# Differential attention in groups of two steps, two sums moved to VectorE, a first load in halves: one change to a whole encoder layer

## The chip, the cores and the metric

The kernel runs on one core of a Trainium2 chip as one program. The metric is the device time of an execution in microseconds. The core has a matrix engine (TensorE, "PE" in the profile; its weight loads are "PEld"), a vector engine (VectorE, "DVE"), an activation engine (ScalarE, "ACT"), a general engine (GpSimd, "POOL") and a queue engine that issues the transfers (SyncE, "SP"). Every engine works through its own instructions in order and waits for the others by semaphores. TensorE writes into PSUM, which has eight banks of 128 x 512 floats.

## The reference

One layer of a hybrid encoder over two sequences of 512 tokens, width 1024, all in float32:

```python
def _layer(x, mem, l, p):
    xn = _rmsnorm(x, p['norm_mix'][l]); mn = _rmsnorm(mem, p['norm_mem'][l])
    u, q, k, v, xq, g = jnp.split(xn @ p['w_in'][l], IN_SPLITS, axis=-1)
    y_s5 = _s5_branch(u, ...)                      # state space branch
    y_diff = _diff_attention(q, k, v, lam, ...)    # q, k rotated
    mk, mv = jnp.split(mn @ p['w_mem_kv'][l], 2, axis=-1)
    y_x = _cross_attention(xq, mk, mv)
    merged = sum(sigmoid(g_n) * (branch_n @ p['w_up'][l, n]))
    x = x + merged @ p['w_out'][l]
    gate, up = jnp.split(_rmsnorm(x, p['norm_ffn'][l]) @ p['w_ffn_in'][l], 2, axis=-1)
    return x + (silu(gate) * up) @ p['w_ffn_out'][l]
```

The differential attention takes, for each of 4 heads, two score maps over 64 channels each, and weighs the values with their difference:

```python
s = jnp.einsum('bqhd,bkhd->bhqk', qblk, k) * scale
probs = softmax(s).reshape(Bn, DIFF_HEADS, 2, Q_BLOCK, L)
w = probs[:, :, 0] - lam * probs[:, :, 1]
out = jnp.einsum('bhqk,bkhe->bqhe', w, v)          # then an rmsnorm over each head's 128 channels
```

## The kernel before

Matrices are kept as two parts of reduced precision, a high part (names ending in h) and the rest (l), and a product is three products on TensorE: high with high, high with low, low with high. `split` (L131) makes the two parts: ScalarE copies the high part, VectorE subtracts it. The kernel is a sequence of stages, whose program order for TensorE is written out by hand while `PE.on` is set; the other engines' orders come from a scheduler at build time, which works with a timeline of its own.

**Start** (L304 to L322). `NWARM` products of zeros run on TensorE while the first transfers are under way. Then the first weight tile is loaded in two halves, and beside each half `mem_part(i)` (L222) loads a tile of two rows of the transposed memory (128 x 2 x 512) and splits each row. `mem_k(0, ...)` multiplies them in the order of the rows.

**Differential attention** (L819 to L922). There are 32 steps: 4 heads x 2 sequences x 4 query tiles of 128 tokens. For each step, `score(i)` (L832) issues six products on half of the rows (64 channels each), two at a time into two banks of the pool "sc", and then the softmax of both: VectorE takes the maximum (L543), ScalarE the exponential with its sum (L548), VectorE combines the two maps (L849, L850) into a tile e. `turn(i)` (L853) transposes e in four pieces into a bank of the pool "tr" and splits it from there: pH on ScalarE, pL on VectorE. `outputs(i)` (L864) multiplies two turned steps with the values, 12 products. After every fourth step `squares` (L884) and `normed` (L897) make the norm over the head's channels; each transposes through a "tr" bank as well.

Between these pieces `fill(n)` (L598) puts products of other work into TensorE's order: it takes units from `queue`, each of six products, until it has given n; what it gives too much is carried to the next call. The queue holds the projections of the next heads' queries and keys with their rotation (VectorE and GpSimd), a half of the values, four gate tiles, and the first two branches of the merge. `finish` draws a unit's generator to its end where a step needs it.

The PSUM pools in this stage are those of the cross attention before it (L584): mm=2 for the filler products, sc=3, tr=2, oo=1 for outputs.

The loop runs one step at a time: score(i + 1), fill, turn(i), outputs for every second step, fill, then squares and normed of earlier steps.

**Feed-forward** (L1057 to L1296). Both its halves multiply in seven instead of eight block products, which needs sums of quarter blocks. `quad_sums` (L966) makes the four sums of a pair of activation tiles: three on VectorE (L971, L973, L974) and one on GpSimd (L972), whose result lies in t_[:, 2]. `quad_split` (L983) splits a pair's tiles and sums. `act_pair` (L1117) loads two tiles that the first half has written to memory and makes their sums. At the seam between the halves, `acts` (L1146) prepares pairs 0 and 1 while the last tile's products run, `nxt` (L1244) pair 2; `pair_in` (L1183) the later ones. `quadrants` (L1104) empties the seven banks of a visit: a ScalarE copy of the first bank (L1107), then VectorE additions (L1101).

Of the kernel before, what the change touches and what calls it, by code (L numbers as in the profile page):

```python
# [14 lines left out]
ALU = mybir.AluOpType  # L15
# [25 lines left out]

NG = (7, 6, 3)

NWARM = 13

SCAN = (40, 47, 53, 60)
ROUND = 12582912.0
# [25 lines left out]
def encoder(ctx: ExitStack, tc: tile.TileContext, a, out):  # L73
    nc = tc.nc
# [18 lines left out]
    def open_banks(**tags):  # L93

        bank_es.close()
        for tag, n in tags.items():
            pools[tag] = bank_es.enter_context(tc.tile_pool(name=tag, bufs=n, space=PSUM, reuse_waits="tile"))
# [28 lines left out]
    def vcol(name, i=0):  # L126
        o = VEC[name][0] + i
        return vec[:, o : o + 1]


    def split(hi, lo, src, scale=None):  # L131

        if scale is None:
            h = S.copy(hi, src)  # L134
            l_ = V.tensor_tensor(out=lo, in0=src, in1=hi.bitcast(F32), op=ALU.subtract)  # L135
        else:
            h = S.activation(out=hi, in_=src, func=AF.Copy, scale=scale)
            l_ = V.scalar_tensor_tensor(out=lo, in0=src, scalar=scale, in1=hi.bitcast(F32), op0=ALU.mult, op1=ALU.subtract)
        return h, l_
# [81 lines left out]

    def mem_part(i):  # L222
        mt_ = slot("ld", [P, 2, L], name="mt")
        nc.sync.dma_start(mt_, a["memT"][:, 2 * i : 2 * i + 2, :])
        for j in range(2):
            split(mh[i][:, j, :], ml[i][:, j, :], mt_[:, j, :], scale=vcol("norm_mem", 2 * i + j))

    last_sq = None
# [369 lines left out]
    def fill(n):  # L598
        nonlocal owed
        owed += n  # L600
        while owed > 0 and queue:
            r = next(queue[0], None)
            if r is None:
                queue.pop(0)
            else:
                owed -= r
        if not queue:
            owed = 0
# [154 lines left out]
    def qk_units(h, is_q):  # L763
        qk[h, is_q], use = rotated(is_q)
        yield from units(a["w_in"][(4 if is_q else 8) + h], xh, xl, use)
# [53 lines left out]
    qk[0, True], use = rotated(True)  # L819
    for s in range(NS):  # L820
        use(s, dq0[s])
    for _ in qk_units(0, False):
        pass
    for _ in gate_units():
# [7 lines left out]
    def score(i):  # L832
        nonlocal last_e
        h, s, qt = steps[i]
        cs = slice(s * L, (s + 1) * L)
        if h and s == qt == 0:
            finish(dk[h])
        if qt == 0:
            s0[h, s] = acol.tile([P, 4], F32, tag="s0", name="s0", bufs=3)
        (qh, ql), (kh, kl), er = qk[h, True], qk[h, False], []  # L840
        qs_ = slice(s * L + qt * P, s * L + (qt + 1) * P)
        sc = [bank("sc") for _ in MAPS]
        for q_, k_ in ((qh, kh), (qh, kl), (ql, kh)):
            for o, rows in zip(sc, MAPS):
                PE.matmul(o, q_[rows, qs_], k_[rows, cs], start=(k_ is kh and q_ is qh), stop=(q_ is ql))
        for mp in range(2):
            er.append(softmax_parts(ap_, acol, sc[mp], L, 1.0, f"d{mp}", None if mp else s0[h, s][:, qt : qt + 1]))
        (e0, sm0), (e1, r1) = er
        V.scalar_tensor_tensor(out=r1, in0=r1, scalar=nlam, in1=sm0, op0=ALU.mult, op1=ALU.mult)  # L849
        last_e = last_x, V.scalar_tensor_tensor(out=e0, in0=e1, scalar=r1, in1=e0, op0=ALU.mult, op1=ALU.add)  # L850
        es[i] = e0

    def turn(i):  # L853
        h, s, qt = steps[i]
        if qt % 2 == 0:
            pT[h, s, qt // 2] = tuple(slot("pT", [P, 4, 2 * P], F32R, n_) for n_ in ("pH", "pL"))
        e0 = es.pop(i)
        tr = aux()
        for j in range(4):
            PE.transpose(tr[:, j * P : (j + 1) * P], e0[:, j * P : (j + 1) * P], ident)  # L860
        ps = slice(qt % 2 * P, qt % 2 * P + P)
        split(*(p_[:, :, ps] for p_ in pT[h, s, qt // 2]), tr.rearrange("p (j q) -> p j q", j=4))

    def outputs(i):  # L864

        h, s, qt = steps[i]
        if h == 2 and s == qt - 1 == 0:
            finish(v1_)
        vh, vl = (v1 if h >= 2 else v0)[s]
        vs = slice((h % 2) * P, (h % 2) * P + P)  # L870
        pH, pL = pT.pop((h, s, qt // 2))
        if qt == 1:
            osb[h, s] = bank("oo")
        od = osb[h, s][:, qt // 2 * 2 * P : (qt // 2 + 1) * 2 * P]
        for j in range(4):
            PE.matmul(od, vh[:, j, vs], pH[:, j, :], start=(j == 0), stop=False)
            PE.matmul(od, vh[:, j, vs], pL[:, j, :], start=False, stop=False)
            PE.matmul(od, vl[:, j, vs], pH[:, j, :], start=False, stop=(j == 3))
        if qt == 3:
            o_ = rp.tile([P, L], F32, tag="nsq", name="osb", bufs=2)  # L880
            S.copy(o_, osb[h, s])
            osb[h, s] = o_
# [14 lines left out]
    def normed(i):  # L897
        h, s, _ = steps[i]
        _, bc = factor(ss[h, s], P, bias=0.0)
        V.scalar_tensor_tensor(out=osb[h, s], in0=osb[h, s], scalar=g04, in1=bc, op0=ALU.mult, op1=ALU.mult)  # L900
        nc.sync.dma_start(bD[1, h, :, s * L : (s + 1) * L], osb[h, s])

    n = len(steps)
    for i in range(-1, n + 3):
        if i + 1 < n:
            score(i + 1)
        if i == 22:
            queue.insert(1, first_in())
        fill(10 if i < n - 1 else 16)
        if 0 <= i < n:  # L910
            turn(i)
        if 0 < i <= n and steps[i - 1][2] % 2:
            outputs(i - 1)
        fill(10)
        if 1 < i <= n + 1 and steps[i - 2][2] == 3:
            squares(i - 2)
        if i > 2 and steps[i - 3][2] == 3:
            normed(i - 3)
    aes.close()
    while queue:  # L920
        fill(24)
# [41 lines left out]

    last_p = None

    def quad_sums(xa_, xb_, tag="ts"):  # L966

        nonlocal last_p
        b11, b12, b21, b22 = xa_[:, 0:L], xa_[:, L:NT], xb_[:, 0:L], xb_[:, L:NT]
        t_ = slot(tag, [P, 4, L], name="ts")  # L970
        V.tensor_tensor(out=t_[:, 0], in0=b12, in1=b11, op=ALU.subtract)  # L971
        last_p = PO.tensor_tensor(out=t_[:, 2], in0=b22, in1=b12, op=ALU.subtract)  # L972
        V.tensor_tensor(out=t_[:, 1], in0=b22, in1=t_[:, 0], op=ALU.subtract)  # L973
        V.tensor_tensor(out=t_[:, 3], in0=b21, in1=t_[:, 1], op=ALU.subtract)  # L974
        return t_
# [138 lines left out]
        c21 = summed(other[0], next(ps), u3, 2)  # L1114
        return c11, summed(other[1], next(ps), u4, 2), c21, c22

    def act_pair(p, tag="ts"):  # L1117

        xa_, xb_ = slot("ld", name="fa"), slot("ld", name="fb")
        nc.sync.dma_start(xa_, aD[2 * p])  # L1120
        nc.sync.dma_start(xb_, aD[2 * p + 1])
        return xa_, xb_, quad_sums(xa_, xb_, tag)

    def all7(i):
        wg = weights4(i)
# [8 lines left out]
    for i in range(KFF):  # L1134
        w = nxt_w or all7(i)
        nxt_w = None
        if i == 1:
            prep = prepare(pes, pieces[NPREP[0] : NPREP[1]])
            next(prep)
        elif i == KFF - 3:  # L1140
            assert next(prep, None) is None
            pes.close()
            open_tags(fes, side="right", tsa=1, tsb=1)
        if i == KFF - 1:
            with tc.issue_after(last_s[1].ins):
                acts = [act_pair(0, "tsa"), act_pair(1, "tsb")]  # L1146
            PE.on = True

        ps = products(i, w)
        p0 = next(ps)  # L1150
        if i == 0:
            for s in range(NS):
                _, bc = rstd(accs[s], DM)
                S.copy(accs[s], bc)
        gf0, gf1, up0, up1 = quadrants(ps, p0)
        ac = ap2.tile([P, NT], F32, tag="ac", name="ac")
        with ExitStack() as es_:
            if i == KFF - 2:
                nxt_w = all7(i + 1)
                es_.enter_context(tc.issue_after(last_s[1].ins))  # L1160
            for s, gf, up in ((0, gf0, up0), (1, gf1, up1)):
                cs = slice(s * L, (s + 1) * L)
                V.tensor_tensor(out=gf, in0=gf, in1=accs[s], op=ALU.mult)
                last_t = S.activation(out=ac[:, cs], in_=gf, func=AF.Tanh, scale=0.5)
                PO.tensor_tensor(out=up, in0=up, in1=accs[s], op=ALU.mult)  # L1165
                V.scalar_tensor_tensor(out=ac[:, cs], in0=ac[:, cs], scalar=1.0, in1=gf, op0=ALU.add, op1=ALU.mult)
                V.tensor_tensor(out=ac[:, cs], in0=ac[:, cs], in1=up, op=ALU.mult)
        nc.sync.dma_start(aD[i], ac)
        if 1 <= i < KFF - 3:
            half_piece((last_t, last_sum))  # L1170
# [70 lines left out]
    next(coming[1])  # L1241
    next(coming[0], None)
    with queued():
        nxt = act_pair(2)  # L1244
    n_p = 0
    for v, (m, lo_, hi_) in enumerate(VISITS):
        ps = [bank() for _ in range(6)] + [aux()]
# [544 lines left out]
```

## Time and profile before

| what | us |
|---|---|
| median of three runs | 1605.7 |
| lowest and highest of them | 1605.64, 1608.26 |
| the profiled execution | 1606.34 |
| its span, first to last instruction | 1604.6 |

The profile is of one execution. A row of a timeline gives an instruction's start and duration in us, its engine and line, its operation, the tile that it writes and the tiles that it reads, its shape, and in brackets how long the engine stood idle before it and what ended that. Names are the program's own: bkmm, bksc, bktr and bkoo are banks of the four PSUM pools. TensorE's products overlap: one lasts about 0.39 us from its first input to its last result, but the next starts 0.23 us after it, so that its pace is read from the starts and its busy time hides small gaps.

### The profile page before, as it was taken

How to read it: one execution, taken by the hardware profiler on the slowest of the kernel's cores; microseconds unless marked ns; L12 is line 12 of the kernel's file. 1: busy time of each engine (PE TensorE's matmuls, PEld its weight loads, DVE VectorE, ACT ScalarE, POOL GpSimd, SP SyncE). 2: the span in 40 equal slices, each digit the busy share in tenths (PEclk: the TensorE clock that was granted, in tenths of full speed). 3: DMA queues.
4: the chain of work that ended last, by engine and by line, in shares of the span. 5: the costliest groups of instructions: out<-in, count | busy, mean ns of one | idle time of the engine just before them, and what ended most of it. 6: DMA issues, size and time to landing. Idle time of an engine off the chain costs nothing.

```text
span 1604.6 us, 21632 instructions
## 1 busy us (share of the span) xinstructions
PE 1587.0 (99%) x7838; PEld 1313.2 (82%) x7838; DVE 1163.7 (73%) x1854; ACT 639.7 (40%) x1142; POOL 557.8 (35%) x451
## 2 busy tenths in 40 slices
PE   9999999999999999999999999999999999999997
PEld 7888788888898778778878878888888888788877
DVE  7976996076773767776465678888898778998664
ACT  6544323274652455574133443232333223233223
POOL 0010100001233220300343367676765556544553
PEclk9999999999999999999999999999999999999999
DMA  9454523576762111244454432333333223985222
GB/s 366 171 160 150 180 95 125 179 272 203 250 223 102 54 47 40 73 158 138 145 190 136 140 118 79 131 118 132 118 112 112 80 91 115 352 323 193 87 66 106
DMA packets 104891, 237.86 MB, mean 148 GB/s; under 512 B 13520, under 2 KB 45008, under 8 KB 104784
## 3 DMA queue, kind: packets, MB, share of 16 engines
q1 hardware_dynamic: 104784, 236.47, 43.2%
q8 instruction: 62, 1.02, 0.3%
q14 instruction: 45, 0.37, 0.1%
HBM read 165.16 MB, written 71.27 MB: 147 GB/s over the span
## 4 chain that ended last, share of the span: by engine, by line
PE 86%; issue 4%; DVE 4%; POOL 3%; DMA 2%; ACT 1%; SPq 0%; POOLq 0%; DVEq 0%; ACTq 0%
PE bkmm L66 74%; PE bksc L66 3%; PE bktr L66 2%; PE bkoo L66 2%; PE bktr L69 2%; DVE tl L135 1%; PE bktr L1626 1%; POOL mg L793 1%; POOL ts L972 1%; PE bktr L1597 1%; DMA yt<-bD 1%; PE bktr L1687 0%; PE bktr L1686 0%; PE bktr L1685 0%; PE bktr L1565 0%
## 5 line engine op out<-in xcount | busy, mean ns | idle before, releaser
L66 PE MATMUL bkmm<-xh,wh 128*128 128x512 f32 x640 | 255.5, 399 | 0.0
L66 PE MATMUL bkmm<-xh,wl 128*128 128x512 f32 x640 | 251.0, 393 | 0.0
L66 PE MATMUL bkmm<-xl,wh 128*128 128x512 f32 x640 | 250.6, 392 | 0.0
L66 PE MATMUL bkmm<-tl,wh 128*128 128x512 f32 (+1 forms) x621 | 241.3, 389 | 1.4 <-DVE tl L135 1.4
L66 PE MATMUL bkmm<-th,wl 128*128 128x512 f32 (+1 forms) x621 | 241.0, 389 | 0.9 <-DVE wl L135 0.9
L66 PE MATMUL bkmm<-th,wh 128*128 128x512 f32 (+1 forms) x621 | 241.2, 389 | 0.0
L134 ACT CAST wh<-wf 128x1024 fp32r<-128x1024 f32 (+1 forms) x134 | 117.9, 880 | 221.9 <-PE bkmm L66 176.8
L135 DVE TENSOR_TENSOR wl<-wf,wh 128x1024 fp32r<-128x1024 f32 (+1 forms) x134 | 146.1, 1090 | 50.2 <-ACT wh L134 45.3
L66 PE MATMUL bkmm<-th,w 128*128 128x512 f32 x432 | 142.7, 394 | 3.2 <-DVE up L1101 1.1
L66 PEld LDWEIGHTS bkmm<-xh,wh 128*128 128x128 f32 x640 | 120.3, 188 | 30.3 <-issue 7.9
L66 PEld LDWEIGHTS bkmm<-xh,wl 128*128 128x128 f32 x640 | 120.3, 188 | 26.7 <-issue 1.3
L66 PEld LDWEIGHTS bkmm<-xl,wh 128*128 128x128 f32 x640 | 120.5, 188 | 22.3 <-issue 0.4
L66 PEld LDWEIGHTS bkmm<-tl,wh 128*128 128x128 f32 x621 | 116.6, 188 | 25.9 <-DVE tl L135 2.2
L66 PEld LDWEIGHTS bkmm<-th,wl 128*128 128x128 f32 x621 | 116.5, 188 | 25.6 <-DVE wl L135 1.8
L66 PEld LDWEIGHTS bkmm<-th,wh 128*128 128x128 f32 x621 | 116.6, 188 | 23.9
L454 POOL TENSOR_TENSOR raw<-raw 128x128 f32<-128x128 f32 x28 | 15.2, 546 | 284.4 <-DVE nb L545 206.5
L1165 POOL TENSOR_TENSOR up<-up,acc 128x512 f32<-128x512 f32 x44 | 84.1, 1931 | 71.4 <-DVE up L1101 71.4
L66 PEld LDWEIGHTS bkmm<-th,w 128*128 128x128 f32 x432 | 80.9, 188 | 26.6 <-DVE up L1101 5.0
L793 POOL TENSOR_TENSOR mg<-mg,gl 128x1024 f32<-128x1024 f32 x16 | 43.5, 2720 | 139.2 <-DVE gl L789 139.2
L548 ACT ACTIVATE e<-bksc,nb 128x512 f32<-128x512 f32 (+1 forms) x96 | 58.7, 615 | 73.7 <-DVE nb L543 51.9
L66 PE MATMUL bkmm<-tl,w 128*128 128x512 f32 x216 | 84.2, 390 | 0.0
L66 PE MATMUL bkmm<-yh,wh 128*128 128x512 f32 x192 | 75.9, 397 | 0.9 <-ACT wh L134 0.6
(640 smaller groups left out, 3541.2 us busy)
## 6 DMA issues: line engine op xcount, KB each, us to landing
wf<-in_w_in SPq DMA_DIRECT2D x40, 512.0 KB, 3.8
wD<-hl SPq DMA_DIRECT2D x28, 512.0 KB, 2.9
w<-wD SPq DMA_DIRECT2D x28, 512.0 KB, 4.5
gD<-gt SPq DMA_DIRECT2D x24, 512.0 KB, 2.8
gl<-gD SPq DMA_DIRECT2D x24, 512.0 KB, 3.4
wf<-in_w_fg SPq DMA_DIRECT2D x22, 512.0 KB, 3.7
wf<-in_w_fu SPq DMA_DIRECT2D x22, 512.0 KB, 3.6
aD<-ac SPq DMA_DIRECT2D x22, 512.0 KB, 3.1
```

Source lines behind the costliest of these rows:

```text
L66: return self.put(self.eng.matmul(*args, **kw))
L69: return self.put(self.eng.transpose(*args, **kw))
L134: h = S.copy(hi, src)
L135: l_ = V.tensor_tensor(out=lo, in0=src, in1=hi.bitcast(F32), op=ALU.subtract)
L454: PO.tensor_tensor(out=a22, in0=a21, in1=a22, op=ALU.add)
L548: last_x = S.activation(out=e, in_=sc, func=AF.Exp, bias=nb, scale=scale, accum_out=sm)
L793: PO.tensor_tensor(out=mg[m], in0=mg[m], in1=gt, op=ALU.add)
L972: last_p = PO.tensor_tensor(out=t_[:, 2], in0=b22, in1=b12, op=ALU.subtract)
L1165: PO.tensor_tensor(out=up, in0=up, in1=accs[s], op=ALU.mult)
L1597: PE.matmul(kp[64 * hf : 64 * hf + 48, g * 144 : (g + 1) * 144], l_[:, 2 * hf + g, :], o_[:, 4 * g4 + 2 * hf + g, :], start=(l_ is lr48), ...
L1626: PE.matmul(ps[:, g * P : (g + 1) * P], w_[:, gg * P : (gg + 1) * P], u_[:, 8 * o + gg, :], start=True, stop=True)
```

## The change

Four edits.

- The attention loop goes in groups of two steps: both scores, then outputs of the group before, then fillers, the two turns with fillers between, fillers, squares. The fillers of a group are 8 + 12 + 10 + 6 + 4 instead of 10 + 10 for each step. Ahead of it the PSUM pools are opened anew with four score banks and one transpose bank.
- `quad_sums` and `act_pair` get an argument for the engine of the fourth sum. Pair 1 (of `acts`) and pair 2 (`nxt`) use VectorE; the others stay on GpSimd.
- The first tile of the memory is loaded row by row, in two transfers.
- 15 instead of 13 products of zeros at the start.

```diff
-NWARM = 13
+NWARM = 15
...
     def mem_part(i):
         mt_ = slot("ld", [P, 2, L], name="mt")
-        nc.sync.dma_start(mt_, a["memT"][:, 2 * i : 2 * i + 2, :])
+        if i:
+            nc.sync.dma_start(mt_, a["memT"][:, 2 * i : 2 * i + 2, :])
         for j in range(2):
+            if i == 0:
+                nc.sync.dma_start(mt_[:, j], a["memT"][:, j, :])
             split(mh[i][:, j, :], ml[i][:, j, :], mt_[:, j, :], scale=vcol("norm_mem", 2 * i + j))
...
         use(s, dq0[s])
+    open_banks(mm=2, sc=4, tr=1, oo=1)
...
     n = len(steps)
-    for i in range(-1, n + 3):
-        if i + 1 < n:
+    for i in range(0, n + 6, 2):
+        if i < n:
+            score(i)
             score(i + 1)
+        if 0 < i <= n:
+            outputs(i - 1)
         if i == 22:
             queue.insert(1, first_in())
-        fill(10 if i < n - 1 else 16)
-        if 0 <= i < n:
-            turn(i)
-        if 0 < i <= n and steps[i - 1][2] % 2:
-            outputs(i - 1)
-        fill(10)
-        if 1 < i <= n + 1 and steps[i - 2][2] == 3:
-            squares(i - 2)
-        if i > 2 and steps[i - 3][2] == 3:
+        fill(8 if i < n else 16)
+        if 2 < i <= n + 2 and steps[i - 3][2] == 3:
             normed(i - 3)
+        if i < n:
+            for j in (i, i + 1):
+                fill(12 if j == i else 10)
+                turn(j)
+            fill(6)
+        if 0 < i <= n and steps[i - 1][2] == 3:
+            squares(i - 1)
+        fill(4 if i < n else 16)
...
-    def quad_sums(xa_, xb_, tag="ts"):
+    def quad_sums(xa_, xb_, tag="ts", third=PO):
...
-        last_p = PO.tensor_tensor(out=t_[:, 2], in0=b22, in1=b12, op=ALU.subtract)
+        last_p = third.tensor_tensor(out=t_[:, 2], in0=b22, in1=b12, op=ALU.subtract)
...
-    def act_pair(p, tag="ts"):
+    def act_pair(p, tag="ts", third=PO):
...
-                acts = [act_pair(0, "tsa"), act_pair(1, "tsb")]
+                acts = [act_pair(0, "tsa"), act_pair(1, "tsb", V)]
...
-        nxt = act_pair(2)
+        nxt = act_pair(2, third=V)
```

More of the change, by code (lines that the diff above doesn't have):

```diff
@@ L1121, in act_pair @@
         nc.sync.dma_start(xb_, aD[2 * p + 1])
-        return xa_, xb_, quad_sums(xa_, xb_, tag)
+        return xa_, xb_, quad_sums(xa_, xb_, tag, third)
     def all7(i):
```

## The prediction

> **What bounds the kernel now.** I read the page first, then TensorE's waits, then the timeline of the three stages that the change touches. From the page, two lines:
>
> ```profile
> span 1604.6 us, 21632 instructions
> PE 1587.0 (99%) x7838; PEld 1313.2 (82%) x7838; DVE 1163.7 (73%) x1854; ACT 639.7 (40%) x1142; POOL 557.8 (35%) x451
> ```
>
> TensorE is busy 99% of the span. So a change counts only where it takes products or gaps out of TensorE's own sequence, or puts gaps in. The list of what TensorE waited for (total, times, longest) is short; its longest rows that lie in the touched stages:
>
> ```profile
> PE bktr L66 <- ACT mh L137: 1.1, 2, 0.7
> PE bkmm L66 <- DVE up L1101: 1.1, 2, 0.6
> PE bkmm L66 <- DVE u L1101: 1.0, 2, 0.6
> ```
>
> The first belongs to the first 10 us, the other two to the seam between the feed-forward's two halves. Nothing of the differential attention stands in the list: no transpose and no score waits there today. The stages as windows (TensorE, weight loads, VectorE, ScalarE, GpSimd):
>
> ```profile
> 520.00:747.00 227.00, 227.00 (x1301) 181.62 (x1300) 159.67 (x304) 126.96 (x290) 36.56 (x24) 1.00 0.24 82
> 1340.00:1400.00 60.00, 57.98 (x249) 46.00 (x248) 53.74 (x65) 18.99 (x24) 35.91 (x16) 1.00 0.71 262
> ```
>
> In attention TensorE never stops for long, VectorE is busy 159.67 of 227 us (70%). At the seam VectorE is busy 53.74 of 60 us (90%) and TensorE loses 2.02 us.
>
> **Attention: what is removed.** "Busy" hides a loss, which the starts show. One score block of before, three pairs of half-row products between full products:
>
> ```profile
> 539.32 0.39 PE L66 MATMUL bkmm<-xh,wl 128*128 128x512 f32 x1
> ...
> 539.64 0.50 PE L66 MATMUL bksc<-rh 64*128 64x512 f32 x2
> ...
> 539.98 0.39 PE L66 MATMUL bksc<-rl,rh 64*128 64x512 f32 x2
> ...
> 540.53 0.50 PE L66 MATMUL bkmm<-xh,wh 128*128 128x512 f32 x1
> ...
> 540.87 0.40 PE L66 MATMUL bkmm<-xl,wh 128*128 128x512 f32 x1
> 541.11 0.39 PE L66 MATMUL bkmm<-xh,wl 128*128 128x512 f32 x1
> ...
> 542.00 1.27 DVE L543 TENSOR_REDUCE nb<-bksc 128x1 f32<-128x512 f32 x2
> ...
> 544.64 0.75 DVE L850 SCALAR_TENSOR_TENSOR e<-e,r 128x512 f32<-128x512 f32 x1
> ```
>
> In a steady run a product follows the last by 0.23 us (540.87 to 541.11). Around the block three starts are late: 539.32 to 539.64 is 0.32, 539.64 to 539.98 is 0.34, 540.53 to 540.87 is 0.34; and from 539.98 the two remaining pairs take 0.55 instead of 0.46. That is 0.09 + 0.11 + 0.11 + 0.09 = 0.40 us of switching for each block, into the half-row form and out again. There are 32 steps, so 32 blocks. The new loop issues score(i) and score(i+1) back to back, in one form, so 16 blocks and 16 switches remain: 16 x 0.40 = **-6.4 us**. I assume that the second block enters as smoothly as pairs within a block do; from 0 to -6.4 are the ends, and I take the whole, since 539.98 is the nearest row: a new pair of the same form, 0.23 after the pair before once the switch is paid. The products themselves stay: both loops hand out 40 filler products for two steps (10 + 10 twice; 8 + 12 + 10 + 6 + 4).
>
> **Attention: what is added.** With sc=4 of eight banks, only one transpose bank is left. A transpose must now wait until ScalarE and VectorE have emptied the one before. Two turns of before, with the ScalarE copy and VectorE subtraction that empty the bank:
>
> ```profile
> 537.71 0.60 PE L69 MATMUL bktr<-ident,e 128*128 128x128 f32 x4
> ...
> 538.07 0.48 PE L66 MATMUL bkmm<-xh,wh 128*128 128x512 f32 x1
> ...
> 538.35 0.59 ACT L134 CAST pH<-bktr 128x512 fp32r<-128x512 f32 x1 [0.26 <-PE bktr L69]
> ...
> 539.00 0.67 DVE L135 TENSOR_TENSOR pL<-bktr,pH 128x512 fp32r<-128x512 f32 x1
> ...
> 543.39 0.60 PE L69 MATMUL bktr<-ident,e 128*128 128x128 f32 x4
> ...
> 546.62 0.67 DVE L135 TENSOR_TENSOR pL<-bktr,pH 128x512 fp32r<-128x512 f32 x1
> ```
>
> The first bank is empty 539.67 - 537.71 = 1.96 us after the transposes began, with nothing in the way; the second 547.29 - 543.39 = 3.90 us, with VectorE on other work. How long does the new order leave? Fillers come six at a time and the overshoot is carried. Following the carry through 16 groups, fill(10) between the two turns gives one unit in 6 groups and two in 10; fill(6) between a second turn and squares gives one unit in 7 of 8 cases. From one set of transposes to the next, one unit leaves 0.36 (537.71 to 538.07) + 0.34 (a first product after a switch, above) + 5 x 0.23 = 1.85 us, two units 3.2 us. So in 13 places the bank is asked for 1.85 us after the last use. At the best chain a wait there is 1.96 - 1.85, about 0.06 to be released (1368.26 to 1368.32 in the seam's rows below) and 0.10 to restart (the late second product above): 0.27, 13 x 0.27 = **+3.5 us**. With the slow chain it is 2.2 us each, +29, and the two-unit places then add 0.9 x 10 = +9. I take the fast end, because the second row is slow for a reason that the regrouping changes: at 543.39 the score block had been issued three us earlier and its softmax held VectorE (542.00 and 544.64). In the new order outputs and at least 18 fillers (4.1 us) lie between the scores and the first turn; the chain of waits has a set of outputs:
>
> ```profile
> 543.99 1.43 PE bkoo L66 x12
> ```
>
> The same distance must hold the softmax. From the end of score(i) to turn(i): 0.69 (three pairs) for score(i+1), 1.43, 4.1, together 6.2 us; before, e was ready at 545.39, 4.9 us after the block ended at 540.53, and the other step's two reductions (1.27) may come in front: 6.2. That just fits; I book 0, with 16 x 1 us as the bad end. A late e holds back TensorE's in-order queue, so outputs and fillers behind the turn wait too. The score banks themselves are free in time: a group is 14 us, their readers need 5 to 7. open_banks before the loop lays the new banks over banks whose readers finished in the cross attention: 0.
>
> By the Trainium skill, TensorEngine Tiling (Array Packing), "PSUM Bottleneck", tiling the rows makes TensorE faster but not the emptying of PSUM, which may then bind. Here four banks instead of two are handed over in 1.8 us; by that rule the 16 us of the bad end, not 0, would be the term, and the whole change would cost +11. The trace so far has VectorE at 70%, which leaves it open.
>
> **The seam: fourth sums on VectorE.** Timelines of GpSimd, VectorE, ScalarE and TensorE around it:
>
> ```profile
> 1353.51 11.81 POOL L972 TENSOR_TENSOR ts<-fb,fa 128x512 f32<-128x512 f32 x1 [5.75 <-DMA fb<-aD]
> ...
> 1374.36 1.74 POOL L972 TENSOR_TENSOR ts<-fb,fa 128x512 f32<-128x512 f32 x1
> ```
> ```profile
> 1362.95 1.22 DVE L135 TENSOR_TENSOR tl<-ts,th 128x1024 fp32r<-128x1024 f32 x1
> 1366.43 1.23 DVE L135 TENSOR_TENSOR tl<-ts,th 128x1024 fp32r<-128x1024 f32 x1 [2.27 <-ACT th L134]
> 1367.58 0.68 DVE L1101 TENSOR_TENSOR u<-bkmm,p 128x512 f32<-128x512 f32 x1
> ...
> 1374.87 1.77 DVE L1163 TENSOR_TENSOR gf<-gf,acc 128x512 f32<-128x512 f32 x1
> ```
> ```profile
> 1365.35 1.05 ACT L134 CAST th<-ts 128x1024 fp32r<-128x1024 f32 x1 [5.10 <-POOL ts L972]
> 1366.31 0.58 ACT L1107 COPY p<-bkmm 128x512 f32<-128x512 f32 x1
> ```
> ```profile
> 1367.51 0.39 PE L66 MATMUL bkmm<-th,w 128*128 128x512 f32 x1
> 1368.32 0.50 PE L66 MATMUL bkmm<-th,w 128*128 128x512 f32 x1 [0.41 <-DVE u L1101]
> ...
> 1371.31 0.50 PE L66 MATMUL bkmm<-th,w 128*128 128x512 f32 x1 [0.64 <-DVE up L1101]
> ```
> ```profile
> 1379.70 0.50 PE L66 MATMUL bkmm<-th,w 128*128 128x512 f32 x1 [0.60 <-DVE u L1101]
> ```
>
> One GpSimd sum of pair 1 took 11.81 us while VectorE ran without a pause to 1364.17. ScalarE stood 5.10 us in front of that sum, the copy of the first bank queued behind it, VectorE's last split came 2.3 us late, and TensorE waited for the banks. On VectorE the sum costs 0.6 us: VectorE then goes on from 1364.17 + 0.6, the last split ends near 1365.9, and the quadrant additions start there instead of at 1367.58, 1.7 us earlier. The waits that end at 1368.32 and 1371.31 go. By the starts the first is 0.81 - 0.23 = 0.58, 0.17 more than the idle time in its row; the second by the same correction 0.64 + 0.17 = 0.81; with 0.1 of restart each, 1.6. The cluster from 1379.70 moves along; there, the GpSimd sum of pair 2, beside the VectorE product that took 1.77 instead of 0.68, goes too, 1.1 saved for 0.6 spent, so of its waits 0.5 goes. Together **-2.1 us**, ends -3.6 and 0 (VectorE's extra 1.3 us eats it).
>
> The Trainium skill, SBUF — State Buffer, "Who interferes with whom", says a VectorE instruction with two SBUF inputs and a GpSimd one that reads SBUF exclude each other. The 11.81 and the 1.77 agree. By it the GpSimd multiplications that stay are blocked by the two sums that move, 2 x 0.68 at most, and the stage would give -0.7 instead.
>
> **The start.** Timeline:
>
> ```profile
> 1.18 4.86 PE L66 MATMUL bktr<-pad_r 128*128 128x128 f32 x26 [1.18 <-DVE pad_r L82]
> ...
> 2.59 1.38 SPq L224 DMA_DIRECT2D mt<-in_memT  x3
> ...
> 5.66 1.33 ACT L137 ACTIVATE mh<-mt,vec 128x512 fp32r<-128x512 f32 x2 [1.17 <-DMA mt<-in_memT]
> ...
> 6.44 0.50 PE L66 MATMUL bktr<-mh,wh 128*128 128x512 f32 x1 [0.41 <-ACT mh L137]
> ...
> 8.62 2.58 ACT L137 ACTIVATE mh<-mt,vec 128x512 fp32r<-128x512 f32 x4 [1.01 <-DMA mt<-in_memT]
> ...
> 9.39 0.50 PE L66 MATMUL bktr<-mh,wh 128*128 128x512 f32 x1 [0.72 <-ACT mh L137]
> ```
>
> The first half row may land before 5.66, but the work that gets done sooner then waits for the next tile, which lands before 8.62 whatever the first does. The end of this stage hangs on 9.39, so the early start is worth 0. The extra issue on SP's queue (0.46 each by the three in 1.38) stands ahead of that tile: +0.46 if the issue sets its landing, 0 if the stream of bytes does. Two more zeros run under the wait that ends at 6.44. I take **0**, ends -0.4 and +0.5.
>
> **Sum.** -6.4 + 3.5 - 2.1 + 0 = -5.0. The profiled execution ran 1606.34 us, 1.7 around its span, and the median of the three is 0.64 below it; 1605.7 - 5.0 = **1600.7**.
>
> **Rivals.** (1) The transpose bank sets the pace: slower. Place: the 13 short distances. It cancels the gains when a wait averages (6.4 + 2.1)/13 = 0.65 us, that is when the bank is emptied later than 2.35 us after the transposes begin. Midway between the two rows (2.93) each waits 1.24: 16.1 - 8.5 = +7.6, so 1613.3. For it: VectorE at 70%, the 3.90. Against: the softmax is farther away. (2) The softmax of two steps comes late, because VectorE and ScalarE get four banks at once: with 0.3 us a group, +4.8, 1605.5; with the bad end of 1 us, 1600.7 + 16 = 1616.7. For it: the 6.2 that just fits. Against: where two filler units more or the norm's transposes lie ahead of the turn, there is 1 to 2 us of room. (3) The switch isn't saved, every score block pays for its new queries: 1605.7 + 3.5 - 2.1 = 1607.1. Against it: pairs in a block follow at the steady rate. (4) No wait at the bank at all, seam at its best: -6.4 - 3.6, so 1595.7.
>
> **Chances.** Forecast 45% (its own range 1598.5 to 1603), rival 1 20%, rival 2 10% mild and 3% at its bad end, rival 3 7%, rival 4 15%. The bound of no change is 0.2%, 3.2 us. Faster: 15 + 43 = 58%; same: 2 + 10 + 7 = 19%; slower: 20 + 3 = 23%. The range 1596 to 1610 leaves out the last edge of rival 4 and the longer part of rivals 1 and 2.
>
> **What would show it.** Right: 16 gaps of 0.4 instead of 32 around the scores; waits of 0.1 to 0.5 us of transposes for pL; no GpSimd sum above 3 us near the seam, additions starting by 1366 counted from the same product. Wrong: rows of TensorE waiting for pL or for e that add up to more than 8 us; 32 switches still there; the first long wait still ending at 9.4 or later shows the start term right.

## The result, and the profile after

The changed kernel runs 1616.54 us (median of 6, 1614.79 to 1616.80) against 1605.65 of the kernel before on the same chip: 1.0062 times as long, interval 1.0049 to 1.0075, 10.9 us slower. Forecast were 1600.7, faster, and a range that ended at 1610.

From its page: the span, the busy time of the engines, and the shares of the chain that ended last.

```profile
span 1614.8 us, 21622 instructions
PE 1585.3 (98%) x7842; PEld 1315.7 (81%) x7842; DVE 1155.1 (72%) x1856; ACT 640.2 (40%) x1142; POOL 545.6 (34%) x449
PE 82%; DVE 5%; issue 4%; POOL 3%; ACT 3%; DMA 3%; SPq 0%; POOLq 0%; DVEq 0%; ACTq 0%
```

TensorE is busy 1.7 us less in a span that is 10.2 us longer: it waits. Where, in us of the two timelines:

| | before | after | this stage |
|---|---|---|---|
| first score of the differential attention | 521.76 | 522.38 | +0.62 |
| last product of the merge | 855.50 | 868.07 | +11.95 |
| first product of the feed-forward's second half | 1366.94 | 1379.38 | -0.13 |
| last of its seven-product visits | 1545.06 | 1554.70 | -2.80 |
| end of the span | 1604.56 | 1614.81 | +0.61 |

The seam gave what was forecast and a little more; the attention, forecast at -2.9, cost 12. The last row's +0.61 goes with the clock: TensorE's granted clock fell to half 9.1 us before the last instruction instead of 5.8; what sets that moment is not shown. Who TensorE waited for (total, times, longest), in the changed kernel:

```profile
PE bktr L69 <- DVE pL L135: 7.0, 6, 1.8
PE bktr L69 <- DVE osb L904: 1.6, 4, 0.6
PE bkoo L66 <- ACT pH L134: 1.6, 1, 1.6
PE bkoo L66 <- DVE pL L135: 1.6, 2, 1.0
PE bkmm L66 <- DMA w<-wD: 1.5, 1, 1.5
...
PE bktr L69 <- DVE r L555: 0.8, 1, 0.8
```

Of these rows only the transfer's belongs to another stage than the attention, and none of them was in the list of before. Transposes wait for pL, the last reader of the bank (6 times), and for the norm's product osb, its last reader after a norm (4 times); outputs wait for what the turns before them should have filled (3 times); once a turn waits for its softmax (r). Together 12.6 us of idle time in 14 waits. The idle time leaves out a little: with the prediction's two corrections, 0.17 by the starts and 0.10 for a late second product, it is 12.6 + 14 x 0.27 = 16.4.

The switches did go: TensorE enters the half-row form of the scores 32 times in the attention of before, and 16 times here. The first group of two scores on TensorE's timeline:

```profile
522.06 0.39 PE L66 MATMUL bkmm<-xh,wl 128*128 128x512 f32 x1
522.38 0.50 PE L66 MATMUL bksc<-rh 64*128 64x512 f32 x2
522.71 0.40 PE L66 MATMUL bksc<-rl,rh 64*128 64x512 f32 x2
522.95 0.40 PE L66 MATMUL bksc<-rh,rl 64*128 64x512 f32 x2
523.18 0.40 PE L66 MATMUL bksc<-rh 64*128 64x512 f32 x2
523.42 0.39 PE L66 MATMUL bksc<-rl,rh 64*128 64x512 f32 x2
```

Late starts stand only at the group's ends; the second score (523.18) follows 0.23 after the last pair of the first.

Why the bank is late: VectorE, ScalarE and GpSimd around the first wait of squares, and TensorE's own rows.

```profile
556.72 0.74 DVE L757 STREAM_SHUFFLE t<-bkmm 128x512 f32<-128x512 f32 x1
557.36 1.22 DVE L135 TENSOR_TENSOR wl<-wf,wh 128x1024 fp32r<-128x1024 f32 x1
558.48 0.69 DVE L135 TENSOR_TENSOR pL<-bktr,pH 128x512 fp32r<-128x512 f32 x1
561.77 0.69 DVE L135 TENSOR_TENSOR rl<-t,rh 128x512 fp32r<-128x512 f32 x1 [2.60 <-ACT rh L134]
562.38 0.68 DVE L135 TENSOR_TENSOR pL<-bktr,pH 128x512 fp32r<-128x512 f32 x1
```
```profile
561.12 0.62 ACT L134 CAST rh<-t 128x512 fp32r<-128x512 f32 x1 [3.83 <-POOL t L759]
561.64 0.58 ACT L134 CAST pH<-bktr 128x512 fp32r<-128x512 f32 x1
```
```profile
559.28 0.60 PE L69 MATMUL bktr<-ident,e 128*128 128x128 f32 x4
563.12 0.66 PE L69 MATMUL bktr<-ident,osb 128*128 128x128 f32 x4 [1.84 <-DVE pL L135]
```

The transposes begin at 559.28 and squares want the bank 1.8 us later. But ScalarE's order has the rotated keys rh first, which wait for GpSimd; pH is held up behind them until 561.64, pL until 562.38. The softmax has no part in this wait. In before rh stood ahead of pH in the same place, and the bank was empty only 4.2 us after the transposes of 557.53; but the next transposes came 7.1 us after these, into the other bank.

In other places it is VectorE whose own order is in the way. After the transposes that begin at 590.96 pH ends at 592.46, but a weight split goes first, and squares wait 1.53 us:

```profile
592.62 1.21 DVE L135 TENSOR_TENSOR wl<-wf,wh 128x1024 fp32r<-128x1024 f32 x1
593.75 0.68 DVE L135 TENSOR_TENSOR pL<-bktr,pH 128x512 fp32r<-128x512 f32 x1
```

A second loss I had not reckoned with at all. Windows of the same place (TensorE, weight loads, VectorE, ScalarE, GpSimd, granted clock, share of the DMA engines, GB/s):

```profile
561.00:564.60 3.60, 1.76 (x14) 1.19 (x14) 1.29 (x2) 2.39 (x10) 0.09 (x1) 1.00 0.10 39
564.70:568.10 3.40, 3.40 (x17) 2.69 (x14) 2.71 (x6) 3.34 (x6) 0.00 (x0) 0.50 0.00 0
568.10:571.50 3.40, 3.40 (x20) 2.87 (x20) 1.97 (x6) 2.47 (x8) 0.00 (x0) 1.00 0.00 0
```

After the stretch with the wait TensorE is granted half its clock for 3.4 us, which costs up to 1.7. Before has no such window between 5 and 1598 us. So the attention's 12 us add up: -6.4 for 16 switches, +16.4 for the waits, up to +1.7 for the clock, 11.7 in all. A stretch of 3.4 us at half clock lowers the mean granted clock of a run of 1615 us by 0.001. Two of the six runs took 1614.8 us and had a mean of 0.998; of the other four, near 1616.6, three had 0.996 or 0.997.

The seam, VectorE and then TensorE:

```profile
1375.00 3.48 DVE L135 TENSOR_TENSOR tl<-ts,th 128x1024 fp32r<-128x1024 f32 x3
1378.41 0.68 DVE L1110 TENSOR_TENSOR u<-bkmm,p 128x512 f32<-128x512 f32 x1
```
```profile
1385.01 0.39 PE L66 MATMUL bkmm<-th,w 128*128 128x512 f32 x1
1386.85 0.50 PE L66 MATMUL bkmm<-th,w 128*128 128x512 f32 x1 [1.46 <-DMA w<-wD]
```

Less the 12.44 by which the stage lies later, the first addition starts at 1365.97; 1365.9 was forecast. The waits for VectorE's additions are gone from the list, and a weight transfer is late next.

### The profile page after: what moved, and what is told of

Read it like the earlier page. It is cut to its first block, busy times and chain, and to the rows that moved or that the text cites. A ratio compares the mean times of both kernels' runs of the same rounds, so it can differ in the third digit from the quotient of the medians.

```text
span 1614.8 us, 21622 instructions
## 1 busy us (share of the span) xinstructions
PE 1585.3 (98%) x7842; PEld 1315.7 (81%) x7842; DVE 1155.1 (72%) x1856; ACT 640.2 (40%) x1142; POOL 545.6 (34%) x449
## 4 chain that ended last, share of the span: by engine, by line
PE 82%; DVE 5%; issue 4%; POOL 3%; ACT 3%; DMA 3%; SPq 0%; POOLq 0%; DVEq 0%; ACTq 0%
PE bkmm L66 72%; PE bktr L66 3%; PE bksc L66 1%; PE bktr L69 1%; PE bkoo L66 1%; DMA yt<-bD 1%; DVE tl L135 1%; PE bktr L1635 1%; POOL mg L796 1%; ACT e L551 1%; POOL t L758 1%; DVE nb L546 1%; POOL t L759 1%; PE bktr L1606 1%; DMA w<-wD 0%
## 5 line engine op out<-in xcount | busy, mean ns | idle before, releaser
L66 PE MATMUL bkmm<-xh,wh 128*128 128x512 f32 x640 | 254.8, 398 | 0.0
L66 PE MATMUL bkmm<-xh,wl 128*128 128x512 f32 x640 | 251.2, 393 | 0.0
L66 PE MATMUL bkmm<-xl,wh 128*128 128x512 f32 x640 | 250.4, 391 | 0.0
L66 PE MATMUL bkmm<-tl,wh 128*128 128x512 f32 (+1 forms) x621 | 241.3, 389 | 1.4 <-DVE tl L135 1.4
L66 PE MATMUL bkmm<-th,wl 128*128 128x512 f32 (+1 forms) x621 | 241.0, 389 | 0.9 <-DVE wl L135 0.9
L66 PE MATMUL bkmm<-th,wh 128*128 128x512 f32 (+1 forms) x621 | 241.2, 389 | 0.0
L66 PE MATMUL bkmm<-th,w 128*128 128x512 f32 x432 | 141.0, 392 | 2.3 <-DMA w<-wD 1.5
L66 PEld LDWEIGHTS bkmm<-xh,wl 128*128 128x128 f32 x640 | 120.2, 188 | 26.7 <-issue 1.3
L66 PEld LDWEIGHTS bkmm<-xh,wh 128*128 128x128 f32 x640 | 120.4, 188 | 22.5 <-ACT gt L635 0.4
L66 PEld LDWEIGHTS bkmm<-xl,wh 128*128 128x128 f32 x640 | 120.5, 188 | 22.4 <-issue 0.4
L66 PEld LDWEIGHTS bkmm<-tl,wh 128*128 128x128 f32 x621 | 116.6, 188 | 26.1 <-DVE tl L135 2.1
L66 PEld LDWEIGHTS bkmm<-th,wl 128*128 128x128 f32 x621 | 116.5, 188 | 25.5 <-DVE wl L135 1.7
L66 PEld LDWEIGHTS bkmm<-th,wh 128*128 128x128 f32 x621 | 116.6, 188 | 23.9
L66 PEld LDWEIGHTS bkmm<-th,w 128*128 128x128 f32 x432 | 81.0, 188 | 22.9 <-DMA w<-wD 1.9
L66 PE MATMUL bkmm<-tl,w 128*128 128x512 f32 x216 | 84.2, 390 | 0.0
L758 POOL TENSOR_TENSOR t<-t,rs 128x512 f32<-128x512 f32 x16 | 27.3, 1705 | 150.0 <-DVE t L757 133.0
L66 PE MATMUL bkmm<-yh,wh 128*128 128x512 f32 x192 | 75.6, 395 | 1.0 <-DVE gl L792 0.9
```

The source lines that it names most:

```text
L66: return self.put(self.eng.matmul(*args, **kw))
L758: PO.tensor_tensor(out=t2, in0=t2, in1=rope[1], op=ALU.mult)
```

## The experiments

Theory: with one transpose bank every transposition waits until the bank is emptied, and its three users (turns, squares, norm) follow each other too closely. Rival: the softmax of two steps comes late. Further rivals came up on the way.

**The loop alone (e1).** The changed kernel with `third=V`, the half loads and the two zeros taken back:

```diff
-NWARM = 15
+NWARM = 13
...
-                acts = [act_pair(0, "tsa"), act_pair(1, "tsb", V)]
+                acts = [act_pair(0, "tsa"), act_pair(1, "tsb")]
...
-        nxt = act_pair(2, third=V)
+        nxt = act_pair(2)
```

> Only the attention loop and its banks are changed; the sums at the seam and the start are those of before. All theories have the loss in the attention: between the first score and the end of the merge TensorE lost 12.0 us against before in the changed kernel, and the seam gave 2.8 us back. Theory (one transpose bank) and its rival (late softmax) both expect 1605.7 + 12 = 1617.6 us; the first products and the seam should lie where they did before (start of the score within 0.1 us of 521.8). Below 1610 would mean that the loss needs the other edits too.

1617.99 us, 1.0073 of before (1.0057 to 1.0088). The first score starts at 521.88, the attention is 12.1 us longer. The loss comes from the loop with its banks, without the other edits.

**The seam alone (e2).** The kernel before with the argument `third` and VectorE for pairs 1 and 2.

> Only the fourth sums of pairs 1 and 2 move to VectorE. If the gain seen at the seam (2.8 us, with a new wait of 1.4 us for a weight transfer in it) is the edit's own: 1605.7 - 2.7 = 1603.0 us. If it came from the shifted time of the stage: 1605 to 1606.

1603.76 us, 0.9984 (0.9974 to 0.9993): a gain of 2.4 us that is the edit's own.

**A second transpose bank (e3).**

```diff
-    open_banks(mm=2, sc=4, tr=1, oo=1)
+    open_banks(mm=2, sc=4, tr=2)
...
         if qt == 1:
-            osb[h, s] = bank("oo")
-        od = osb[h, s][:, qt // 2 * 2 * P : (qt // 2 + 1) * 2 * P]
+            osb[h, s] = rp.tile([P, L], F32, tag="nsq", name="osb", bufs=2)
+        od = aux()[:, : 2 * P]
...
-        if qt == 3:
-            o_ = rp.tile([P, L], F32, tag="nsq", name="osb", bufs=2)
-            S.copy(o_, osb[h, s])
-            osb[h, s] = o_
+        S.copy(osb[h, s][:, qt // 2 * 2 * P : (qt // 2 + 1) * 2 * P], od)
```

> The changed kernel with two transpose banks: outputs takes its bank from the transposes' pool and its half is copied out at once (16 copies of 128x256 instead of 8 of 128x512), so that no bank is kept for outputs. Theory (transposes wait for the one bank): the waits for pL and for the norm's product, about 11 us, go, the 16 switches stay saved: 1602 to 1606 us. Rival (late softmax): the waits move from the bank to the tile e, 1612 or more. No third score block should cost more than in the changed kernel.

1604.83 us, 0.9990 (0.9980 to 0.9999). The ten runs fall into two groups: five from 1601.62 to 1603.65 with a mean granted clock of 0.997 or 0.998, five from 1606.01 to 1606.71 with 0.995 or 0.996. The profile is of the second group. TensorE's list of waits:

```profile
PE bktr L66 <- DVE pL L135: 2.0, 2, 1.0
...
PE bktr L66 <- ACT pH L134: 1.7, 1, 1.7
...
PE bktr L69 <- DVE r L555: 0.8, 1, 0.8
```

No transposition waits for a bank any more (the rows of L66 are outputs, which now write to the same pool). The attention is 0.7 us longer than before instead of 12.0. The single wait for the softmax is as it was, so the rival falls. What is left is outputs, put straight behind the scores, with the turns before them not yet split, and 3.4 us of half clock from 693.83 on, up to 1.7 us of the attention.

**The same fillers, spread otherwise (e4).**

```diff
-        fill(8 if i < n else 16)
+        fill(6 if i < n else 16)
-                fill(12 if j == i else 10)
+                fill(8 if j == i else 12)
-            fill(6)
+            fill(12)
-        fill(4 if i < n else 16)
+        fill(2 if i < n else 16)
```

> The changed kernel with its 40 fillers a group given as 6 + 8 + 12 + 12 + 2 instead of 8 + 12 + 10 + 6 + 4: always two units (3.2 us) between the two turns and between a turn and squares, one unit or so less between the scores and the first turn. Theory (distance between uses of one bank): the waits for pL of 0.4, 2.0, 1.1, 1.7, 1.1 and 1.7 us fall to 0.3 us or less each where the bank was emptied within 3.3 us, 5 to 7 us gained: 1610 to 1612 us. Rival (late softmax): the first turn comes 1.4 us sooner after its scores and waits for e in most groups, 1618 or more.

1620.57 us, 1.0089 (1.0074 to 1.0104), runs from 1618.29 to 1622.78, of which the profile has the fastest. The theory's 1610 to 1612 is missed. The rival's time came, 1618 or more, but not by the rival's way. The waits:

```profile
PE bktr L69 <- DVE osb L904: 11.4, 7, 2.4
...
PE bktr L69 <- DVE pL L135: 1.8, 3, 0.8
...
PE bktr L69 <- DVE r L555: 0.8, 1, 0.8
```

With 3.2 us between turns the waits for pL fall from 7.0 to 1.8 us, near to what the theory said; the norm, which now has fewer products between it and the next turn, holds the bank instead and rises from 1.6 to 11.4. Two of these waits, 2.2 and 2.4 us, are followed by 3.4 us of half clock each. Turns come sooner after their scores and still wait only once for the softmax. One bank has three users, and room given to one is taken from another.

**Two more (e5, e7).** The changed kernel with the rotation's GpSimd products on VectorE (`PO.tensor_tensor` to `V.tensor_tensor` in `rotated`), against the idea that ScalarE's wait for GpSimd is what makes the bank late:

> The changed kernel with the rotation's two products (GpSimd) moved to VectorE. Theory (ScalarE stands in front of the rotated tile, which GpSimd finishes late, with pH queued behind): the copies pH start 0.7 us after their transposes also where squares follow, and the waits of squares for pL (2.0, 1.7 and 1.7 us) fall below 0.7 each, 3 to 4 us gained less what 22 us more of VectorE's work costs. Rival (VectorE's own load makes pL late): those waits grow.

One run, 1618.31 us, and the first row of its waits:

```profile
PE bktr L69 <- DVE pL L135: 7.0, 6, 1.9
```

The total did not move. The wait of squares shown above fell from 1.84 to 0.45 us, as the idea had it; the two that follow in squares, 1.53 and 1.52 before, grew to 1.92 each, as its rival had it: there VectorE was on a weight split and now on the rotation's product too, ahead of pL. And the kernel before, its loop untouched, with the new banks alone (`open_banks(mm=2, sc=4, tr=1, oo=1)` ahead of the loop):

> The kernel before with the new banks alone (four score banks, one transpose bank), its loop by single steps. Theory (one bank is emptied late): waits for pL and the norm's product appear here too, though turns are 7 us apart, because squares, norm and turns still follow each other by 2 to 3 us: +3 to +8 us in the attention. Rival (the loss belongs to grouping): below +1 us.

One run, 1621.13 us:

```profile
PE bktr L69 <- DVE pL L135: 9.6, 7, 3.9
```

The attention is 15.0 us longer than before, more than theory had said, with half clock for 10.2 us of it. In this one run the single bank by itself costs more than the whole change does; grouping is not the cause.

**Two banks and later outputs (e6).** e3 with the start of before, and outputs behind the first fillers:

```diff
-        if 0 < i <= n:
-            outputs(i - 1)
         if i == 22:
             queue.insert(1, first_in())
         fill(8 if i < n else 16)
+        if 0 < i <= n:
+            outputs(i - 1)
```

> The loop in groups with two transpose banks as in e3, outputs after the first fillers instead of straight after the scores, the sums at the seam on VectorE, the start of before. Theory (bank reuse and the early outputs are all that costs): the 5 us of waits that e3 still had at outputs go, the switches stay saved: attention 4 to 6 us shorter than before, with the seam's 2.5 about 1598 us. Rival (the scores' switches are not worth 6.4, or two steps' softmax costs as much elsewhere): 1602 to 1604.

1602.93 us, 0.9981 (0.9972 to 0.9990), faster than either kernel, though not the 1598 hoped for: the profiled execution has a span of 1598.6, the runs go from 1600.09 to 1604.66. In its trace the attention is 2.1 us shorter than before; the waits for outputs are gone, and two turns wait 3.1 us for a late e, where ScalarE and VectorE split the next branch's tiles. But the median gain, 2.4 us against before, is no larger than that of the seam alone (e2), which e6 contains. By the medians the new loop gains nothing; the 2.1 us are those of one execution, among the shortest of the eleven.

**The scores apart (e9).** e6 with `fill(6)` between the two scores and 2 instead of 8 behind them:

> e6 with six fillers taken from behind the two scores and put between them, nothing else. If the saving of the grouping is the switch into and out of the half-row form (0.40 us a block), the 16 switches come back and the attention is 6.4 us longer than in e6: its time about 1605 to 1609 beside e6's 1600 to 1603, and 32 late pairs stand in the trace. If the gain of e6 over the changed kernel is all from the banks and the order of outputs: within 2 us of e6.

1606.53 us, 1.0010 of before (1.0001 to 1.0019). From first score to the last product of the merge it takes 336.8 us against 331.7 in e6, 5.1 more, though its turns wait less:

```profile
PE bktr L69 <- DVE r L552: 1.6, 3, 0.7
```

With 1.5 us less of waits, 16 switches cost 5.1 + 1.5 = 6.6 us, or 6.3 with 0.27 for the one wait more. Neither trace has half clock in the attention. That term of the forecast, 6.4, is shown, by one trace of each.

**The start alone (e8), and with its pause filled (e10).** The kernel before with the half loads and 15 zeros; then with ten more zeros after the second row's products:

> The kernel before with the first rows in halves and 15 zeros alone. From the traces of the runs so far: the second tile lands 0.5 us or more later behind the extra issue, and where the pause before it is longest the granted clock halves for some us: +0.6 to +2.9 us, 1606.3 to 1608.6. If the profiles differ there only by chance between executions: 1605.7.

1606.13 us, 1.0005 (0.9996 to 1.0013), runs from 1604.08 to 1608.11: no verdict on the mean. Its trace, TensorE's timeline and two windows:

```profile
8.12 0.40 PE L66 MATMUL bktr<-mh,wl 128*128 128x512 f32 x1
10.03 0.51 PE L66 MATMUL bktr<-mh,wh 128*128 128x512 f32 x1 [1.51 <-ACT mh L137]
```
```profile
8.00:11.30 3.30, 1.51 (x5) 0.71 (x5) 1.98 (x3) 2.43 (x5) 0.00 (x0) 1.00 1.00 381
11.40:14.80 3.40, 3.40 (x10) 2.61 (x9) 3.27 (x6) 2.80 (x4) 0.00 (x0) 0.50 1.07 399
```

The early row's products are done early, the next tile lands later (10.03 against 9.39 in before), the pause between them is 1.5 us, and half clock follows: the first score comes 2.2 us later. The late tile is no accident of this trace: its products start between 9.0 and 9.5 us in the seven traces with the old start, and between 10.0 and 11.0 in the five with the new one alone (this one, the changed kernel, e3, e4, e5).

> The start edit alone (first rows in halves, 15 zeros) with ten more products of zeros in the pause behind the second row's products. Theory (the pause of TensorE lets its granted clock fall to half for 3.4 us): no half clock before 20 us and the runs lose their upper group, 1605 to 1606 in all runs, beside 1604.1 to 1608.1 without the zeros. Rival (the spread comes from the transfers alone): 1604 to 1608 again, with the first score at +2 us in the slow ones.

1606.45 us, 1.0005 (0.9996 to 1.0014), 1606.04 to 1608.10. No half clock in its trace:

```profile
11.40:14.80 3.40, 3.40 (x17) 2.75 (x16) 3.32 (x6) 2.90 (x5) 0.00 (x0) 1.00 1.05 390
```

But ten zeros were too many: they held the next products until 10.93, so the short times went too; and two of the eleven runs took 1607.24 and 1608.10 with no lower clock than the rest (0.998), so neither expectation is met. In e8 the four runs from 1607.56 on had a mean granted clock of 0.997, and five of the seven others 0.998, which points to the clock for these. Whether the spread of e8 is the clock or the transfers stays open.

**e6 once more (e11).**

> The same kernel as e6, for a second profile. e6's runs fell into two groups, about 1600.4 and 1603.3. Theory (half-clock windows of 3.4 us after pauses in the attention, 1.7 us each): a time near 1603 goes with one or two such windows in the trace, a time near 1600.4 with none. Rival (transfers): the difference lies before the first score or at the seam.

1602.75 us. Its trace has two windows of half clock, each behind a stretch with a wait:

```profile
722.00:725.30 3.30, 1.28 (x9) 1.14 (x9) 3.23 (x9) 2.80 (x7) 0.00 (x0) 1.00 0.48 159
725.40:728.70 3.30, 3.30 (x9) 2.52 (x9) 1.92 (x3) 0.00 (x0) 0.00 (x0) 0.50 0.70 238
1370.00:1373.80 3.80, 1.47 (x7) 0.92 (x6) 3.65 (x6) 3.42 (x6) 0.09 (x1) 1.00 1.02 411
1373.90:1377.20 3.30, 3.30 (x9) 2.52 (x9) 3.19 (x6) 2.39 (x3) 0.00 (x0) 0.50 1.03 420
```

e6's first profile, 2.4 us shorter, has none. The difference lies at the seam: 2.3 us of waiting for a weight transfer instead of 1.6, and the half clock behind it. That the other runs near 1603 are of this kind is likely, not shown: of e6's six runs from 1602.9 on three had a mean granted clock of 0.996, of the five below none had less than 0.997.

## Why the prediction was wrong, step by step

- **The switches, -6.4: right.** 16 late entries instead of 32, and 6.6 us by e9.
- **The single bank, +3.5: this step failed.** Its 13 places were right, and the changed kernel's trace has all of them. In eight the next transposes came 0.15 to 0.32 us after the 1.85 that I had reckoned, about as forecast. In the other five they came 1.1 to 2.0 us after it. Together that is 9.3 us instead of 3.5. And I counted the places where a turn had come before, but not those behind the norm (4 waits, 1.6 us). As rows of the list, the waits for the bank came to 8.6 us of idle time, 10 of them, 11.3 with restarts.
- **Why I took the fast row.** I had two rows for emptying the bank, 1.96 and 3.90 us, and took the fast one, on the ground that the slow one came from the softmax, which the regrouping moves away. That ground was half of the truth. In the trace of before the softmax of another step holds ScalarE or VectorE for 0.5 us or more ahead of pH or pL in 21 of the 32 turns, in the changed kernel in one, and the median time until the bank is empty falls from 3.76 to 2.11 us. But rotations, weight splits and other work that comes with the fillers stand there for 0.5 us or more in 12 turns of either trace, because ScalarE's and VectorE's orders are fixed (3.78 us for the turn at 559.28). The slow row of before shows both, pH and then VectorE up to pL:

```profile
544.05 0.58 ACT L134 CAST pH<-bktr 128x512 fp32r<-128x512 f32 x1
545.38 0.68 DVE L752 TENSOR_TENSOR t<-bkmm,rc 128x512 f32<-128x512 f32 x1
545.99 0.73 DVE L754 STREAM_SHUFFLE t<-bkmm 128x512 f32<-128x512 f32 x1
```

  pH ended at 544.63, the softmax's combination held VectorE until 545.39, and then two operations of the rotation until 546.62. The prediction named the first and left out the second.
- **Outputs: not costed.** I moved them ahead in the list of the change and did not ask what they wait for. Three waits, 3.2 us idle, 4.0 with restarts; e6 removes them.
- **The softmax, 0: nearly right.** One wait of 0.8 us, 1.1 with its restart; the distance of 6.2 us just held, as forecast. The rule of the Trainium skill that was set against it (TensorEngine Tiling (Array Packing), "PSUM Bottleneck") does not show here: no row of the list waits for a score bank. At the transpose bank emptying does bind, but there because one bank is left, not because TensorE became faster.
- **The clock: not considered.** Up to 1.7 us in the profiled execution. With 7.8 more for the bank, 4.0 for outputs and 1.1 for the softmax that is 14.6 of the 14.9 us by which the attention missed its -2.9.
- **The seam, -2.1: right in mechanism, -2.8 in the trace,** -2.4 alone in e2.
- **The start, 0 with ends -0.4 and +0.5:** +0.6 in the trace of the changed kernel, beyond the bad end. With the extra issue the products of the next tile start at least 0.5 us later than in before, in all five traces that show it; the pause before it, which half clock can follow, was not in the sum.
- Rival 1 had place and mechanism, with 1613.3 for the midway bank, and 20%. The rows gave no reason to weigh it below the forecast: the bound that I had worked out, an emptying later than 2.35 us, was exceeded by one of the two rows quoted, and by 24 of the 32 turns in the trace of before. Only five were empty within 2 us.

## What to carry to other kernels

When a pool of buffers shrinks, list all its users in their new order and set each distance against every emptying in the trace, not against the fastest. Of each slow one, list all the work that stood ahead of it, and ask which of it the change moves: here the softmax went and the rotations and weight splits stayed. A latency that costs nothing while a second buffer hides it is not tuned, and stays long. A merge of blocks that saves switches pays only if the buffers it takes are not the ones that hide another engine's order; here the same grouping with the buffer found elsewhere took the loss of 12 us away, and whether it gains anything beyond the seam's 2.4 us the medians don't show.

## What the runs showed of the hardware

A wait of TensorE can cost more than its length. In eight of the thirteen traces the granted clock fell to 0.50 before the last 20 us, 13 times in all, for 3.41 us each (once for 6.83), and each time right behind 3.41 us in which TensorE was busy 0.7 to 1.6 us. Within a trace these falls keep a common beat: in the five traces that have two, the second starts 8, 9, 32, 190 and 200 times 3.413 us after the first. The Trainium skill, TensorE: Matmul & The Clock Gate, "Part 1: The HAM clock gate", has a monitor that looks at windows of about 3.4 us that run freely; the length and the common beat agree with it. The advice of the Trainium skill, TensorE: Matmul & The Clock Gate, "Why this matters for your kernels", to leave no idle gaps above some 3 us is too mild for these traces: single waits of 1.5 to 2.4 us were enough. Where a wait falls matters too. One of 3.2 us for a weight transfer in e5 lay across two stretches of the beat, with 1.70 and 1.95 us busy in them, and no half clock followed. But the beat and the busy time do not settle it alone: e6 has a wait of 2.15 us in a stretch with 1.47 us busy, and nothing followed; why not is open.

GpSimd's sum of before that took 11.81 us, where the same sum took 1.3 to 1.8 elsewhere, ran beside a whole row of VectorE instructions with two SBUF inputs and ended 1.15 us after that row, whose last instruction ended at 1364.17. That it got no turn within the row is read from these times. Moved to VectorE the sum took 0.68.
